# A two-layer decoder trunk: the out-projection's PSUM banks are filled with the residual ahead of the matmuls, the signs of the seven products are turned, and normed tiles are scaled whole

## The chip, the cores and the metric

The kernel runs on one core of a Trainium2 chip. The metric is the device time of one execution in microseconds (us), as the median of several runs. A profiled execution gives a trace beside it: every instruction of the engines with its start and duration, and every transfer with its issue and landing. The engines are TensorE (PE in the profile, PEld its weight loads), VectorE (DVE), ScalarE (ACT), GpSimd (POOL) and SyncE (SP), whose queue issues most loads.

## The reference

One sequence of 256 tokens with 2048 channels goes through two layers, all in float32. Cut to what matters:

```python
for l in range(DEPTH):                       # 2
    h = _rmsnorm(x, attn_norm_g[l])
    q, k, v, gate_b, gate_c, conv_in = jnp.split(h @ w_in[l], splits, axis=-1)   # 6 x 1024
    ...
    attn = _diff_attention(q, k, v, lam, rel_bias)       # then a norm per head
    conv = gate_b * _short_conv(gate_c * conv_in, conv_w[l])
    x = x + jnp.concatenate([attn, conv], axis=-1) @ w_out[l]
    hm = _rmsnorm(x, mlp_norm_g[l]) @ w_up[l]            # 2048 x 8192
    x = x + jnp.square(jax.nn.relu(hm)) @ w_down[l]      # 8192 x 2048
```

The change touches the norms, the projections of q and k, the out-projection (`w_out`) and the MLP.

## The kernel before

**Precision.** Every float32 operand is split into a high part and a rest (`hi`, `lo`), and a product is three matmuls: hi by hi, hi by lo, lo by hi. ScalarE makes the high part (a copy into the type that TensorE reads), VectorE the rest (a subtraction). For weights: a load (`raw`, `uraw`, `draw`), then `whi`/`uhi` (L341, L1291), then `wlo`/`ulo` (L342, L1292). For `w_up` one load of 1 MB holds two columns of 128 for half of k (`kh`), and is split in two steps, one for each column.

**Seven products.** At the indices listed in the plans (`FIRST`, `SECOND`, `LEFT`, `RIGHT`, `SEVEN_AT`) a 2 by 2 block of blocks is multiplied with seven products instead of eight. That needs sums of the activations' quarters (`sums_of`, L846: four VectorE operations of 128x128 into `sv`, then its hi and lo parts `sf`; in the MLP `square`, L1452 to L1455) and sums of the weights' quarters (`sums` in `jobs`, L910 to L924: `w7t`, four operations of 128x512; its first two are split into `w7x`, its last two into `w7y`; `w7b` is the split of the weights themselves). The products go into PSUM banks `prods[1]` to `prods[8]`; some of them end up in one block of the result and some are added in afterwards (`results`, L964 to L982).

**The out-projection.** Its left half (two chunks of 512 output channels, `left`) is worked beside the last columns of the gate, and the right half (`right`) follows. Banks `prods[2]`, `prods[3]`, `prods[4]`, `prods[8]` collect ordinary products and products of the seven. At the end VectorE adds each bank to the residual `xs` (L1061, L1167, four tiles of 128x512 per half), and four partial sums `e1` to `e4` to it (L980), after one addition straight from `prods[5]` (L975). The partial sums lie in a place of 4 KB of pool `tmp` (tag "ao"), one of `nat`, and one of `kpool` (tag "kL", 2 KB used).

**The norms.** `chunk` (L517) transposes a 512-channel tile of `xs` on TensorE, and, for pairs that aren't among the first sevens, `split_gained` (L304) makes hi on ScalarE (L307, scaled copy, 128x256) and lo on VectorE (L309). Of other pairs a scaled tile `ny` is made whole, then split (L540 to L543) and summed. `squares` (L555) makes the sums of squares on ScalarE (`junk`, L559).

**The MLP.** Column pair i of `w_up` is multiplied for both tokens' tiles (PE L1427: `up` is the first pair, `upw` the second, `upc` the rest), evicted, squared (`square`), and two pairs later multiplied with `w_down`. Its pools open where the pools of the attention part closed, so a load of `w_up` must wait until the last reader of that memory is done: the pools `upa`, `upb` and `upc` (L1269 on) take turns, and lie over `rpool`, `tmp`, `kpool` and others.

**Order.** TensorE's instructions are in program order. The other engines and SyncE's queue are ordered by the scheduler of the framework, which keeps the priority of the program and a model of when memory comes free; each queue is worked strictly in its order. `work.tick()` moves pieces of other work between matmuls; `late` and `issue_after` pin some instructions.

Of the kernel before, what the change touches and what calls it, by code (L numbers as in the profile page):

```python
# [133 lines left out]
def trunk(ctx: ExitStack, tc: tile.TileContext, x, w_in, w_out, conv_w, q_norm_g, k_norm_g,  # L134
# [370 lines left out]

    class Norm:
# [10 lines left out]
        def chunk(self, n, wait):  # L517
# [5 lines left out]
            for j in range(2):  # L523
# [9 lines left out]
                if self.sums_of is None or pair not in SEVEN_FIRST[self.l]:  # L533
                    split_gained(a, *((2 * j + i, tp[:, i * S:(i + 1) * S], scales[i])
                                      for i in range(2)))
                else:
                    y = wide(f"ny{pair}").rearrange("p (k s) -> p k s", k=2)
                    for i in range(2):
# [5 lines left out]
                    self.sums_of(pair, *(y[:, i, t * P:(t + 1) * P]  # L544
                                         for i in range(2) for t in range(NT)))
# [288 lines left out]
    A11, A21, A12, A22, S1, S2, S3, S4 = range(8)  # L834

    class BySeven:
# [9 lines left out]
        def sums_of(self, i, a11, a21, a12, a22):  # L846

            if i < self.rooms_of:
# [3 lines left out]
                hi, lo = (self.rooms[i % 2][:, part] for part in range(2))  # L852
            else:
# [11 lines left out]
        def jobs(self, w, i, cols, in_keys=False):  # L865
# [44 lines left out]
            def sums():  # L910
                left, right = mine["raw"]
                pool, tag = (self.kpool, "kL") if in_keys else (self.pool, "b")
                t = mine["t"] = pool.tile([P, 4, CH], F32, tag=tag, name="w7t")

                with behind(in_keys or self.rooms_of == 8):
                    nc.vector.tensor_sub(t[:, 0], right[:, 0], left[:, 0])
# [4 lines left out]
                nc.vector.tensor_add(t[:, 2], t[:, 1], left[:, 0])  # L921
                nc.vector.tensor_sub(t[:, 3], left[:, 1], t[:, 2])
                return made
# [7 lines left out]
        def form(self, i, pa, a):  # L931

            if a >= S1:
                return self.sums[i][pa][:, a - S1]
# [3 lines left out]
        def product(self, n, i, a, b, start, stop):  # L938

            for m, (pa, pw) in enumerate(TERMS):  # L940
                nc.tensor.matmul(self.prods[n], self.form(i, pa, a), b[pw],  # L941
                                 start=(start and m == 0), stop=(stop and m == 2))

        def pair(self, i, chunks, starts=(), last=False):

            for n, accs in chunks:
                hi, lo = self.weights.take()
                for j in range(2):
# [8 lines left out]
                    for t, pa, pw in steps:  # L957
# [3 lines left out]
                            stop=(last and j == 1 and (pa, pw) == TERMS[-1]))  # L961
                    work.tick()

        def results(self, n):  # L964
# [3 lines left out]
            x11, x21, x12, x22 = (xs[n + m][:, t] for m in range(2) for t in range(NT))  # L968
# [9 lines left out]
            def add():  # L978
                for x_, e in ((x11, e1), (x21, e3), (x12, e4), (x22, e3)):
                    nc.vector.tensor_add(x_, x_, e)  # L980

            return add  # L982
# [15 lines left out]
        def left(self, acts, cv):  # L998
# [8 lines left out]
            def column(c):  # L1007
# [8 lines left out]
                if c % 2 and i in SEVEN_LEFT + SEVEN_RIGHT:  # L1016
                    self.sums_of(i, *(y[:, k, t * P:(t + 1) * P]
                                      for k in range(2) for t in range(NT)))

            def banks():  # L1020
# [3 lines left out]
                for n in (5, 7, 4):  # L1024
                    prods[n] = bank(f"po{l}{n}")

            for j, (what, i) in enumerate(LEFT):
# [4 lines left out]
                elif what == "a":  # L1032
# [5 lines left out]
                    self.product(2, i, A12, b21, start, not {"a", 0} & rest)  # L1038
                    self.product(3, i, S4, b22, start, not {"a", 1} & rest)
                    self.product(5, i, S1, self.t1, start, end)  # L1040
                    work.tick()
                elif what == "b":
# [5 lines left out]
                    if end:  # L1048
                        add = self.results(0)
                else:  # L1050
                    opening = what == 1 and 8 not in prods
                    if opening:
                        prods[8] = ps.tile([P, CH], F32, tag="av", name=f"po{l}8", bufs=1)
# [699 lines left out]
```

## Time and profile before

| | |
|---|---|
| median of 3 runs | 2112.55 us (2112.5 to 2112.66) |
| span of the profiled execution | 2110.7 us |
| TensorE busy | 2105.2 us |
| VectorE busy | 1834.6 us |
| ScalarE busy | 1407.5 us |
| GpSimd busy | 189.4 us |
| read from and written to HBM | 440.52 MB and 33.58 MB |

The span runs from the first instruction of the profiled execution to its last; the page gives no other time of that execution, and the median of the runs stands 1.85 us above it. A row of the timeline gives the start and the duration of an instruction in us, its engine and line, what it writes and reads, and in brackets how long the engine sat idle before it and what ended that. A row of the groups gives the total busy time in us and the mean in ns, then the idle time before them. The chain that ended last is followed back from the last instruction to what released each.

### The profile page before, as it was taken

The numbers are of one execution on the slowest core, as the hardware profiler recorded it, in microseconds if no ns is written. First come the engines' busy times: TensorE is split into PE (matmuls) and PEld (weight loads), VectorE is DVE, ScalarE is ACT, GpSimd is POOL, SyncE is SP. The second block draws the span as 40 slices with busy tenths as digits, with TensorE's granted clock in tenths as the row PEclk, the third lists the DMA queues.
The fourth block names the chain that finished last, engine by engine and source line by source line (L and its number), as shares of the span: only waits on it lengthen the run. The fifth ranks groups of instructions, "written<-read, shape, count | busy, mean of one in ns | idle before, by whom it ended". The sixth has DMA issues, their size and how long they took to land.

```text
span 2110.7 us, 29252 instructions
## 1 busy us (share of the span) xinstructions
PE 2105.2 (100%) x10809; PEld 1799.0 (85%) x10809; DVE 1834.6 (87%) x2525; ACT 1407.5 (67%) x1823; POOL 189.4 (9%) x226
## 2 busy tenths in 40 slices
PE   9999999999999999999999999999999999999999
PEld 7888888888888888888888888888888888888887
DVE  7888788898888888799888887988988888888998
ACT  6777566676776766666566775657676677675664
POOL 2211120000000000011101121000000000000110
PEclk9999999999999999999999999999999999999999
DMA  7655575887777777789566456668777777777993
GB/s 265 205 154 167 171 216 182 289 259 229 230 238 229 231 232 230 251 291 310 171 220 188 152 170 185 195 193 290 255 238 229 229 230 238 230 229 260 315 309 113
DMA packets 312607, 476.01 MB, mean 226 GB/s; under 512 B 12723, under 2 KB 209669, under 8 KB 312464
## 3 DMA queue, kind: packets, MB, share of 16 engines
q1 hardware_dynamic: 284752, 406.76, 60.7%
q0 software_dynamic: 27520, 67.24, 10.1%
q8 instruction: 85, 1.39, 0.3%
q14 instruction: 58, 0.48, 0.1%
q10 hardware_dynamic: 192, 0.15, 0.0%
HBM read 440.52 MB, written 33.58 MB: 225 GB/s over the span
## 4 chain that ended last, share of the span: by engine, by line
PE 98%; DMA 1%; POOL 1%; DVE 1%; issue 0%; ACT 0%; ACTq 0%; DVEq 0%
PE upc L1427 31%; PE pr L1470 14%; PE dn L1551 8%; PE gc L481 4%; PE ci L481 4%; PE gb L433 4%; PE v L456 3%; PE q L958 3%; PE o L958 3%; PE k L958 3%; PE dn L1470 3%; PE po L941 2%; PE dn L1645 2%; PE pr1r L1470 2%; PE pr0r L1470 2%; PE po L958 2%
## 5 line engine op out<-in xcount | busy, mean ns | idle before, releaser
L1427 PE MATMUL upc<-nT,uhi 128*128 128x512 f32 x1920 | 454.7, 389 | 0.0
L1427 PEld LDWEIGHTS upc<-nT,uhi 128*128 128x128 f32 x1920 | 360.2, 188 | 74.7
L1292 DVE TENSOR_TENSOR ulo<-uraw,uhi 128x1024 fp32r<-128x1024 f32 x256 | 312.3, 1222 | 109.8 <-ACT f L1459 91.5
L341 ACT ACTIVATE whi<-raw 128x1024 fp32r<-128x1024 f32 x232 | 244.7, 1058 | 180.2 <-issue 21.8
L1291 ACT ACTIVATE uhi<-uraw 128x1024 fp32r<-128x1024 f32 x256 | 270.6, 1057 | 135.7 <-PE upc L1427 115.4
L342 DVE TENSOR_TENSOR wlo<-raw,whi 128x1024 fp32r<-128x1024 f32 x232 | 284.3, 1234 | 53.1 <-ACT whi L341 46.9
L1427 PEld LDWEIGHTS upc<-nT,ulo 128*128 128x128 f32 x1920 | 246.2, 191 | 9.4
L1427 PE MATMUL upc<-nT,ulo 128*128 128x256 f32 x1920 | 249.1, 283 | 0.0
L1317 ACT ACTIVATE bh<-draw 128x1536 fp32r<-128x1536 f32 x86 | 128.3, 1492 | 103.7 <-PE pr L1470 82.1
L1318 DVE TENSOR_TENSOR bl<-draw,bh 128x1536 fp32r<-128x1536 f32 x86 | 151.3, 1759 | 11.4 <-ACT bh L1317 10.9
L1551 PE MATMUL dn<-whi,fb 128*128 128x512 f32 x480 | 152.0, 389 | 0.0
L1470 PE MATMUL pr<-bh,f 128*128 128x512 f32 x360 | 121.4, 391 | 0.0
L341 ACT ACTIVATE whi<-uraw 128x1024 fp32r<-128x1024 f32 x60 | 63.7, 1062 | 72.0 <-PE dn L1551 58.5
L1437 ACT ACTIVATE ev<-upc 128x512 f32<-128x512 f32 x120 | 72.0, 600 | 54.0 <-PE upc L1427 54.0
L1317 ACT ACTIVATE t24h<-t 128x1024 fp32r<-128x1024 f32 x86 | 91.4, 1063 | 23.7 <-PE pr L1470 15.9
L1551 PEld LDWEIGHTS dn<-whi,fb 128*128 128x128 f32 x480 | 90.1, 188 | 18.6
L1318 DVE TENSOR_TENSOR t24l<-t,t24h 128x1024 fp32r<-128x1024 f32 x86 | 104.9, 1220 | 0.2
L1330 DVE TENSOR_TENSOR t<-draw 128x1024 f32<-128x1024 f32 x86 | 105.0, 1221 | 0.1
L1318 DVE TENSOR_TENSOR t13l<-t,t13h 128x1024 fp32r<-128x1024 f32 x86 | 104.9, 1220 | 0.0
L1317 ACT ACTIVATE t13h<-t 128x1024 fp32r<-128x1024 f32 x86 | 91.5, 1063 | 8.1 <-DVE t L1330 2.9
L1470 PE MATMUL pr<-t13h,f 128*128 128x512 f32 x240 | 93.8, 391 | 0.0
L1551 PE MATMUL dn<-wlo,fb 128*128 128x512 f32 x240 | 93.4, 389 | 0.0
(528 smaller groups left out, 4383.9 us busy)
## 6 DMA issues: line engine op xcount, KB each, us to landing
uraw<-in_w_up_dram SPq DMA_DIRECT2D x128, 1024.0 KB, 6.3
raw<-in_w_in_dram SPq DMA_DIRECT2D x191, 512.0 KB, 4.2
draw<-in_w_down_dram SPq DMA_DIRECT2D x180, 512.0 KB, 5.3
raw<-in_w_out_dram SPq DMA_DIRECT2D x64, 512.0 KB, 4.5
uraw<-in_w_down_dram SPq DMA_DIRECT2D x60, 512.0 KB, 6.8
hid0p<-f POOLq DMA_DIRECT2D x17, 512.0 KB, 3.5
fb<-hid0p POOLq DMA_DIRECT2D x17, 512.0 KB, 8.0
hid1p<-f POOLq DMA_DIRECT2D x17, 512.0 KB, 3.5
```

What stands on the lines that cost most here:

```text
L341: pair = (nc.scalar.activation(hi, raw, AF.Copy), nc.vector.tensor_sub(lo, raw, hi.bitcast(F32)))
L342: nc.vector.tensor_sub(lo, raw, hi.bitcast(F32)))
L481: nc.tensor.matmul(acc[:, f, 0] if part else acc[:, f], wt[:, k % 4, fs], a.ap[:, 0, k % KG] if part else a.ap[:, :, k % KG], start=(part ...
L958: nc.tensor.matmul(accs[t], a.ap[:, pa, k % KG, t * P:(t + 1) * P], (hi, lo)[pw][:, j], start=(j == 0 and (pa, pw) == (0, 0) and (n, t) in ...
L1291: pair = (nc.scalar.activation(hi, src, AF.Copy), nc.vector.tensor_sub(lo, src, hi.bitcast(F32)))
L1292: nc.vector.tensor_sub(lo, src, hi.bitcast(F32)))
L1317: keep(nc.scalar.activation(hi, src, AF.Copy))
L1318: keep(nc.vector.tensor_sub(lo, src, hi.bitcast(F32)))
L1330: keep(nc.vector.tensor_sub(t[:, 0:2], raw[:, 0::2], raw[:, 1::-1]))
L1427: nc.tensor.matmul(acc[:, 0] if part else acc, wt[part][:, k], a.ap[:, 0, k % KG] if part else a.ap[:, :, k % KG], start=(part == 0 and kh ...
L1470: nc.tensor.matmul(prods[n], f[:, pa, a], b[pw], start=(start and m == 0), stop=(stop and m == 2))
L1551: nc.tensor.matmul(prods[p], f[:, pa, 2 * k + t], b[pw][:, n], start=(p in starts and k == 0 and m == 0), stop=(stop and k == 1 and m == 2))
```

## The change

Five things are changed.

1. *Seeds.* ScalarE copies the residual `xs` into the out-projection's banks before their first matmul (`seed`), and these matmuls accumulate onto it (`start` false). The additions at the end are then `xs = bank + e`, and those of `xs` alone (L980, L975) go, except one for the left half.
2. *Room.* The partial sums of `results` lie in one place of 8 KB of `kpool` (tag "kL") in place of `tmp`.
3. *Signs.* The two sums S1 and S3 are turned so that the sums of quarters are two differences at one go, in `sums_of` and in the MLP's `square`: three operations in place of four (128x256 once, 128x128 twice). The weights' sums become additions. Where the signs of products 5, 6 or 7 turn, the additions of the results become subtractions.
4. *Order of w7t.* In q and k (`rooms_of == 8`) the last two sums of `w7t` are made before `w7x` is split.
5. *Norm tiles scaled whole.* All norms but the very first make `ny` and split it as one tile of 128x512: three copies on ScalarE and one subtraction on VectorE in place of two and two.

```diff
@@ class Norm, chunk @@
-                if self.sums_of is None or pair not in SEVEN_FIRST[self.l]:
+                if not at_once and (self.sums_of is None or pair not in SEVEN_FIRST[self.l]):
...
@@ class BySeven @@
-    A11, A21, A12, A22, S1, S2, S3, S4 = range(8)
+    A11, A21, A12, A22, S3, S1, S2, S4 = range(8)
...
-            nc.vector.tensor_add(v[:, 0], a21, a22)
-            nc.vector.tensor_sub(v[:, 1], v[:, 0], a11)
-            nc.vector.tensor_sub(v[:, 2], a11, a21)
-            nc.vector.tensor_sub(v[:, 3], a12, v[:, 1])
+            if both is None:
+                nc.vector.tensor_sub(v[:, 0], a11, a21)
+                nc.vector.tensor_sub(v[:, 1], a21, a22)
+            else:
+                nc.vector.tensor_sub(v[:, 0:2], *both)
+            nc.vector.tensor_sub(v[:, 2], v[:, 1], a11)
+            nc.vector.tensor_add(v[:, 3], a12, v[:, 2])
...
+                def rest():
+                    nc.vector.tensor_add(t[:, 2], t[:, 0], right[:, 1])
+                    nc.vector.tensor_add(t[:, 3], left[:, 1], t[:, 2])
+
                 with behind(in_keys or self.rooms_of == 8):
-                    nc.vector.tensor_sub(t[:, 0], right[:, 0], left[:, 0])
-                    nc.vector.tensor_sub(t[:, 1], right[:, 1], right[:, 0])
+                    nc.vector.tensor_add(t[:, 0], left[:, 0], right[:, 0])
+                    nc.vector.tensor_add(t[:, 1], right[:, 0], right[:, 1])
                 room = self.biasp.tile([P, 2, 2, CH], F32R, tag=self.spare, name="w7x")
+                if self.rooms_of == 8:
+                    rest()
                 made = two(room, t[:, 0:2])
...
+        def seed(self, *places):
+
+            for n, t, acc in places:
+                nc.scalar.activation(acc, xs[n][:, t], AF.Copy)
...
-            room = self.tmp.tile([P, 2, CH], F32, tag="ao", name="es", bufs=1)
-            e1, e2, e3 = room[:, 0], wide("e2"), room[:, 1]
-            e4 = self.kpool.tile([P, CH], F32, tag="kL", name="es4")
+            x21 = xs[n][:, 1]
+            room = self.kpool.tile([P, 4, CH], F32, tag="kL", name="es")
+            e1, e3, e4, e5 = (room[:, m] for m in range(4))
+            e2 = wide("e2")
             nc.scalar.activation(e1, prods[1], AF.Copy)
             nc.vector.tensor_add(e2, prods[6], e1)
-            nc.vector.tensor_add(e4, prods[5], e2)
-            nc.vector.tensor_add(x22, prods[5], x22)
+            nc.vector.tensor_sub(e4, prods[5], e2)
             nc.vector.tensor_add(e3, prods[7], e2)
...
+            nc.vector.tensor_sub(e5, prods[5], e3)
+            if n == 0:
+                nc.vector.tensor_add(x21, x21, e3)
+                e3 = x21
+            return (e1, e3), (e4, e5)
...
@@ right @@
+            for n in range(2):
+                self.seed(*((2 + n, t, accs[n][t]) for t in range(NT)))
...
                 if not {"s", what} & rest:
                     for t in range(NT):
-                        nc.vector.tensor_add(xs[2 + what][:, t], accs[what][t], xs[2 + what][:, t])
-                    if add is not None:
-                        add()
-                        add = None
+                        nc.vector.tensor_add(xs[2 + what][:, t], accs[what][t], e[what][t])
...
@@ mlp @@
-                    keep(nc.vector.tensor_sub(t[:, 0:2], raw[:, 0::2], raw[:, 1::-1]))
+                    keep(nc.vector.tensor_add(t[:, 0:2], raw[:, 1:3],
+                                              raw[:, 0:1].to_broadcast([P, 2, CH])))
...
-                    nc.vector.tensor_add(h[:, S1], h[:, A21], h[:, A22])
+                    nc.vector.tensor_sub(h[:, S3:S1 + 1], h[:, A11:A21 + 1], h[:, A21:A22 + 1:2])
                     nc.vector.tensor_sub(h[:, S2], h[:, S1], h[:, A11])
-                    nc.vector.tensor_sub(h[:, S3], h[:, A11], h[:, A21])
-                    nc.vector.tensor_sub(h[:, S4], h[:, A12], h[:, S2])
+                    nc.vector.tensor_add(h[:, S4], h[:, A12], h[:, S2])
```

In the left half banks 2 and 3 are seeded when they are opened (`banks`) and bank 8 when its first pair opens it; bank 4 is not, and the one addition to `xs` stands for it. The orders of TensorE and GpSimd are the same in both programs. Two places of the others follow, each before and after; the line numbers after are those of the changed file.

SyncE's queue from the last loads of `w_out` (`raw`) into the MLP of layer 0, before. `uraw` are loads of `w_up`, in the order pair 0 first half, pair 0 second half, pair 1 first half, pair 1 second half, pair 2 first half; `draw` are loads of `w_down`:

```order
L383 DMA raw<-in_w_out_dram 128x2x512 x10
L895 DMA raw<-in_w_out_dram 128x2x512 x2
L383 DMA raw<-in_w_out_dram 128x2x512 x2
L895 DMA raw<-in_w_out_dram 128x2x512 x2
L383 DMA raw<-in_w_out_dram 128x2x512 x4
L1284 DMA uraw<-in_w_up_dram 128x8x256 x5
L1302 DMA draw<-in_w_down_dram 128x1024 x6
L1284 DMA uraw<-in_w_up_dram 128x8x256 x5
```

And after, the same stretch:

```order
L383 DMA raw<-in_w_out_dram 128x2x512 x6
L1298 DMA uraw<-in_w_up_dram 128x8x256
L383 DMA raw<-in_w_out_dram 128x2x512 x4
L906 DMA raw<-in_w_out_dram 128x2x512 x2
L383 DMA raw<-in_w_out_dram 128x2x512 x2
L906 DMA raw<-in_w_out_dram 128x2x512 x2
L383 DMA raw<-in_w_out_dram 128x2x512 x4
L1298 DMA uraw<-in_w_up_dram 128x8x256 x3
L1316 DMA draw<-in_w_down_dram 128x1024 x3
L1298 DMA uraw<-in_w_up_dram 128x8x256
L1316 DMA draw<-in_w_down_dram 128x1024 x3
L1298 DMA uraw<-in_w_up_dram 128x8x256 x5
```

The second half of pair 1 has moved up among the loads of `w_out`; the three `uraw` are both halves of pair 0 and the first half of pair 2; the lone one between the `draw` is the first half of pair 1. The queue has the same order in layer 1.

VectorE at the first seven of q and k in layer 1, before:

```order
L916 TENSOR_TENSOR w7t<-raw 128x512
L917 TENSOR_TENSOR w7t<-raw 128x512
L880 TENSOR_TENSOR w7b<-raw,w7b 128x1024
L880 TENSOR_TENSOR wlo<-raw,whi 128x512
L921 TENSOR_TENSOR w7t<-w7t,raw 128x512
L880 TENSOR_TENSOR w7x<-w7t,w7x 128x1024
L922 TENSOR_TENSOR w7t<-raw,w7t 128x512
L342 TENSOR_TENSOR wlo<-raw,whi 128x1024
L880 TENSOR_TENSOR w7y<-w7t,w7y 128x1024
L342 TENSOR_TENSOR wlo<-raw,whi 128x1024
```

And after:

```order
L931 TENSOR_TENSOR w7t<-raw 128x512
L932 TENSOR_TENSOR w7t<-raw 128x512
L872 TENSOR_TENSOR sv_10049<-ny_10044,sv_10049 128x128
L891 TENSOR_TENSOR w7b<-raw,w7b 128x1024
L891 TENSOR_TENSOR wlo<-raw,whi 128x512
L927 TENSOR_TENSOR w7t<-w7t,raw 128x512
L874 TENSOR_TENSOR sf<-sv_10049,sf 128x512
L928 TENSOR_TENSOR w7t<-raw,w7t 128x512
L891 TENSOR_TENSOR w7x<-w7t,w7x 128x1024
L342 TENSOR_TENSOR wlo<-raw,whi 128x1024 x2
L891 TENSOR_TENSOR w7y<-w7t,w7y 128x1024
```

The fourth sum of `w7t` and the end of the other seven's sums (`sv`, `sf`) now stand ahead of `w7x`, and both `wlo` ahead of `w7y`.

More of the change, by code (lines that the diff above doesn't have):

```diff
@@ L504, in rstd_of, with quarters_of @@
         return r, power
+    def quarters_of(y):
+        q = y.rearrange("p k (t c) -> p (k t) c", c=P)
+        return *(q[:, m] for m in range(4)), (q[:, 0:2], q[:, 1:4:2])
     class Norm:
@@ L852, in sums_of @@
                 hi, lo = (self.rooms[i % 2][:, part] for part in range(2))
+            elif i % 2:
+                room = self.tmp.tile([P, 2, 4, P], F32R, tag="ao", name="so", bufs=1)
+                hi, lo = (room[:, part] for part in range(2))
             else:
@@ L1048, in left @@
                     if end:
-                        add = self.results(0)
+                        e = self.results(0)
                 else:
```

63 lines of the change are left out of this document (28 added, 35 removed).

## The prediction

> **What bounds the kernel now.** I read the page first: its busy times, the row of the granted clock and the chain that ended last.
>
> ```profile
> span 2110.7 us, 29252 instructions
> PE 2105.2 (100%) x10809; PEld 1799.0 (85%) x10809; DVE 1834.6 (87%) x2525; ACT 1407.5 (67%) x1823; POOL 189.4 (9%) x226
> PEclk9999999999999999999999999999999999999999
> PE 98%; DMA 1%; POOL 1%; DVE 1%; issue 0%; ACT 0%; ACTq 0%; DVEq 0%
> ```
>
> The reader is to see that TensorE is busy in 2105.2 of 2110.7 us, at the full granted clock in every slice, and that 98% of the chain is TensorE following itself. Next I asked for all waits of TensorE, which is a list of four:
>
> ```profile
> PE warm L189 <- DVE mhalf L181: 1.1, 1, 1.1
> PE q L958 <- ACT whi L368: 0.4, 1, 0.4
> PE tpb L570 <- DMA x<-in_x_dram: 0.2, 1, 0.2
> PE k00tp L688 <- DVE ke L660: 0.2, 1, 0.2
> ```
>
> They add up to 1.9 us in the whole span. The change leaves TensorE's instructions and their order as they are, so the most that removed waits can return is 1.9 us, which is 0.09% of the time. A measurement of this kernel can tell a difference of about 0.2%, 4.2 us, from none. The question is therefore whether a stall of more than 4.2 us appears. Last I read the chain around the places where instructions move, for the rate of TensorE:
>
> ```profile
> 359.73 5.44 PE o L958 x24
> ```
>
> 24 matmuls of 512 columns take 5.44 us, 0.2267 us each.
>
> **What costs nothing.** The change takes work off VectorE and puts some on ScalarE. Counted in the two programs, VectorE loses 130 operations of 128x128 and 44 scaled differences of the norm, and gains 65 of 128x256 and 8 of 128x512; ScalarE gains 36 copies of 128x512 (14 seeds, 22 in the norm). The groups:
>
> ```profile
> L1453 DVE TENSOR_TENSOR h<-h 128x128 f32<-128x128 f32 x60 | 17.2, 286 | 0.0
> L309 DVE SCALAR_TENSOR_TENSOR nT<-tpn,gains,nT 128x256 fp32r<-128x256 f32 x32 | 13.9, 478 | 1.1 <-ACT nT L307 1.1
> L980 DVE TENSOR_TENSOR x<-x,es 128x512 f32<-128x512 f32 x16 | 10.4, 685 | 0.0
> L559 ACT ACTIVATE junk<-x 128x512 f32<-128x512 f32 x32 | 19.8, 622 | 2.6 <-DVE e L1524 2.0 <-DVE x L980 0.6
> ```
>
> For a 128x256 operation I take 0.42 us, an estimate between 0.286 for 128 columns and 0.685 for 512. VectorE: 130 x 0.286 + 44 x 0.478 - 65 x 0.42 - 8 x 0.685 = 25 us less; ScalarE 36 x 0.622 = 22 us more. Neither sets the end, since TensorE waits for either only in the four rows above. That is the cover, and it must hold at each place. In the MLP, where 120 of the 128x128 operations turn into 60 of 128x256, it does: nothing is added on ScalarE, and there was no wait to remove.
>
> The seeds are new instructions that TensorE must wait for. A copy into PSUM I price at the 0.622 us of the copy above (bounds: 0.53, half of the 1.06 us of 1024 columns at 328.63 below, and 0.69, VectorE's 512-column add). The tightest are those of the right half of the out-projection and of bank 8:
>
> ```profile
> 315.58 5.44 PE po L958 x24
> 336.76 5.44 PE o L958 x24
> ...
> 315.75 0.63 ACT L879 ACTIVATE whi<-raw 128x512 fp32r<-128x512 f32 x1 [0.20 <-DMA raw<-in_w_out_dram]
> 328.63 1.06 ACT L341 ACTIVATE whi<-raw 128x1024 fp32r<-128x1024 f32 x1 [2.80 <-PE po L958]
> ...
> 336.31 1.88 DVE L1061 TENSOR_TENSOR x<-po,x 128x512 f32<-128x512 f32 x3
> ```
>
> Bank 8 opens half-way through the 24 matmuls at 315.58, at 318.3; its seed stands on ScalarE behind the split at 315.75, which ends at 316.4, so it is there at 317.0, 1.3 us early. The first two right seeds fit into the 2.80 us in which ScalarE idled before 328.63, 8 us before 336.76. The other two wait for banks that the adds at 336.31 free at 338.2 (and by then ScalarE has the four squares of 0.622 us to make); I put them at 339.6 and 341.3, and they are needed after the 24 matmuls and a group of transposes, at 342.6 at the earliest. At each place the slack is over 1.2 us; a seed at the dear end costs 0.07 us more. I count zero.
>
> **Term 1: the loads at the start of each MLP.** This is where the change costs. The four partial sums of `results` (L968) move out of their place in `tmp` into one 8 KB place of `kpool`. Memory of `tmp` comes free early, that of `kpool` late, and the uploads of the MLP's first weights use both. In the order of SyncE's queue one 1 MB load (of the second pair of columns, second half of k) goes forward among the loads of w_out; its partner, the first half of k, falls from third place to behind the load of the third pair and three loads of w_down. Before, these were (the answers for single loads: how long the issue took, when it was, how long to the landing):
>
> ```profile
> L1284 SPq DMA_DIRECT2D uraw<-in_w_up_dram x1: 367/367/367, 370.0 to 370.0; - x1
> DMA to landing us min/median/max: 6.6/6.6/6.6
> ...
> L1284 SPq DMA_DIRECT2D uraw<-in_w_up_dram x1: 367/367/367, 372.8 to 372.8; - x1
> DMA to landing us min/median/max: 9.2/9.2/9.2
> ...
> L1284 SPq DMA_DIRECT2D uraw<-in_w_up_dram x1: 367/367/367, 379.7 to 379.7; - x1
> DMA to landing us min/median/max: 5.9/5.9/5.9
> ...
> L1284 SPq DMA_DIRECT2D uraw<-in_w_up_dram x1: 368/368/368, 380.7 to 380.7; - x1
> DMA to landing us min/median/max: 8.3/8.3/8.3
> ...
> L1302 SPq DMA_DIRECT2D draw<-in_w_down_dram x6: 424/481/1532, 381.5 to 385.1; - x6
> DMA to landing us min/median/max: 8.7/9.8/11.9
> ```
>
> The first load, at 370.0, takes 6.6 us. The load in question is issued at 372.8 and lands at 382.0. Those at 379.7 and 380.7 land at 385.6 and 389.0, 3.5 apart, both being in flight; the six of w_down land from 381.5 + 8.7 = 390.2 to 385.1 + 11.9 = 397.0, 1.36 us apart. Who uses what:
>
> ```profile
> 376.66 1.06 ACT L1291 ACTIVATE uhi<-uraw 128x1024 fp32r<-128x1024 f32 x1 [2.91 <-DMA uraw<-in_w_up_dram]
> 387.58 1.06 ACT L1291 ACTIVATE uhi<-uraw 128x1024 fp32r<-128x1024 f32 x1 [0.23 <-PE up L1427]
> ...
> 379.50 1.22 DVE L1292 TENSOR_TENSOR ulo<-uraw,uhi 128x1024 fp32r<-128x1024 f32 x1
> 380.86 1.29 DVE L1167 TENSOR_TENSOR x<-o,x 128x512 f32<-128x512 f32 x2
> ...
> 393.99 3.82 PE L1427 MATMUL upw<-nT,uhi 128*128 128x512 f32 x16
> ```
>
> Its split into uhi (1.06 us) ran at 387.58, and TensorE used it at 393.99: 5 us in hand. After, ScalarE makes both squares (`junk`) between the first two splits, so VectorE's second difference moves from 379.50 to about 380.0 and ends at 381.2, which releases the load of the third pair. With nothing ahead of it in flight it should take about as long as the two fastest, 5.9 and 6.6, say 6.3: landing at 387.5. Three loads of w_down at 1.36 bring 391.6, and the load in question, 1 MB or two such steps, lands at 394.3 (its own memory, which holds the partial sums until the last adds, about those at 380.86 with 1.29 us, now ending at 382.3, is free before its turn). Split in 1.06, TensorE starts at about 395.35: 1.35 us late. The layer has a second, smaller delay in the same stretch: norm tiles are scaled whole, so the last lo half of the normed tiles comes later, about 0.5 us over its due time. That lies ahead of the same wait and vanishes in it. The cheap end: 5.9 and steps a tenth of a us shorter give 393.4 and a stall of 0.5; the dear end: 6.6, steps a tenth longer and the 3.5 for the 1 MB give 395.7 and 2.8. I take the middle, since the queue is full behind the first load as it was in the rows. Layer 1 has the same order of loads; two layers make 2.7 us. What stands behind the waiting split on ScalarE is the partner's split and the first split of w_down, both due over 1 us after.
>
> **Term 2: the first seven of layer 1.** In q and k the two later sums of `w7t` now stand ahead of the differences of w7x:
>
> ```profile
> 1078.72 0.69 DVE L916 TENSOR_TENSOR w7t<-raw 128x512 f32<-128x512 f32 x1 [0.73 <-DMA raw<-in_w_in_dram]
> 1079.93 1.22 DVE L880 TENSOR_TENSOR w7b<-raw,w7b 128x1024 fp32r<-128x1024 f32 x1
> 1085.22 1.23 DVE L880 TENSOR_TENSOR w7y<-w7t,w7y 128x1024 fp32r<-128x1024 f32 x1
> ...
> 1083.80 0.68 PE po1r L941 x3
> ```
>
> VectorE starts at a landing, 1078.72, so earlier savings don't help. Two 512-column operations lie between the first two rows, 1.21 us, so one starts 0.6 after another, 0.08 before its 0.685 are over; with the same overlap it is 1.14 for 1024 columns and 0.2 for 128. The new order: two sums 1.2, one 128-column sum 0.2, w7b 1.14, half of wlo 0.6, third sum 0.6, the low half of sf 0.6, fourth sum 0.6, w7x 1.14, two wlo 2.28, and w7y ends 1.23 after it starts: 1088.3. TensorE wants it with the 17th matmul after 1083.80, at 1083.80 + 16 x 0.2267 = 1087.4. Stall 0.9 us (0 if one wlo slips behind, 1.3 if ScalarE's whi for the second wlo is late).
>
> **Term 3: the seven of layer 0** was late already:
>
> ```profile
> 41.16 1.22 DVE L880 TENSOR_TENSOR w7y<-w7t,w7y 128x1024 fp32r<-128x1024 f32 x1
> 41.96 1.20 PE L941 MATMUL po0r<-w7y,sf 128*128 128x512 f32 x3
> 38.53 1.04 ACT L879 ACTIVATE w7y<-w7t 128x1024 fp32r<-128x1024 f32 x1
> ```
>
> The second of its three matmuls was due 0.2267 after 41.96, at 42.2, and the low half came at 42.4. ScalarE now makes w7y (before at 38.53) behind a copy of about 0.6 us and a split that waits for TensorE, which ends it at some 41.1 and the low half at 42.7: 0.3 us more (0 to 0.6).
>
> The sum is 2.7 + 0.9 + 0.3 = 3.9 us; against the span of 2110.7 that is 2114.6. The profile gives its execution's span alone, and the median of the runs, 2112.55, stands 1.85 us above it; with that, 2116.4. The bounds are 2 x 0.5 = 1.0 and 2 x 2.8 + 1.3 + 0.6 = 7.5 us, so 2113.5 to 2120.
>
> **The rivals.** *The load is in time.* If the load in question doesn't queue behind the others' bytes but takes the shortest time in the rows from its own issue (some 384.3: after 381.2, one issue of 1.53 and three of about 0.5 us), it lands at 384.3 + 5.9 = 390.2, is split by 391.3, and term 1 is zero: 2112.55 + 1.2 = 2113.75. For it: the load at 379.7 took 5.9 us though that of 372.8 was still in flight. Against: six loads of w_down landed 1.36 apart and waited up to 11.9 us.
>
> The Trainium skill, "SBUF — State Buffer", section "The DMA setup-cost knee", fits a load's time as about 2 us and its bytes over 436 GB/s; by it a 1 MB load takes an estimated 4.4 us, the landings come earlier and this rival holds. The trace disagrees, with 5.9 us for the fastest of these rows.
>
> *The load is later: slower.* The place is the same, the first upw of each MLP. If the landing is at 395.7 (the dear end), the two layers lose 5.6 and all is 2112.55 + 5.6 + 1.2 = 2119.35. It decides from 4.2 us in all, which is a stall of 1.5 us in each layer, a landing at 394.45 instead of 394.3. For it: this is hardly later than my estimate, and landings 3.5 apart occur. Against: with nothing in flight ahead of it the first load should be at the fast end.
>
> *VectorE's relief counts: faster.* If only waits go, 1.9 us at most: 2110.65, within 0.2%. Should TensorE's row hide waits for VectorE, up to the 25 us taken from it could return: 2087.5. Against it: 0.2267 us per matmul in 24 at 315.58, 336.76 and 359.73 alike, whatever VectorE did beside.
>
> The Trainium skill, "Perfetto Trace Analysis", section "Identifying the Most-Contended Engine", calls the busy share of matmuls a poor measure, and judges by the weight loads. By that rule the 85% of PEld would leave room for this rival; the even rate in the trace speaks against it.
>
> **How the numbers follow.** Forecast, with the middle sizes: 0.42. Load in time: 0.14. Load later: 0.38. Relief within the four waits: 0.04, beyond them: 0.02. Faster by over 0.2% is the last, 0.02; slower by over 0.2% is the third, 0.38; within 0.2% is the rest, 0.60. The likeliest is 2116.4. From 2112.6 to 2120 all but the relief (0.06) and the upper end of the late load (about 0.1) lie inside.
>
> **What would show it.** Right: in the waits of TensorE of the changed kernel new rows of upw on ACT uhi, about 1.35 us, twice; a row of po1r on DVE w7y of 0.9; PE's busy time unchanged; the load of term 1 landing near 394.3, about 10 us after issue. Wrong: upw starts right behind up without a gap; or a wait of TensorE at a place not named here, on a seed above all; or a chain with less than 2105 us of TensorE.

## The result and the profile after

The changed kernel takes 2123.85 us, median of 4 runs (2123.08 to 2124.59). The kernel before took 2112.61 us in the same session (2112.5 to 2114.92). The ratio is 1.0051, with an interval of 1.0039 to 1.0064: slower, by 11.2 us. Forecast were 2116.4 us and "within 0.2%", with a range up to 2120; the rival "the load is later" stood at 2119.35. The time lies outside the range, above both. The profiled execution took 2123.08 us, its span is 2121.3 us, 10.6 more than the 2110.7 of before.

The page of the changed kernel, in the rows that were shown of before:

```profile
span 2121.3 us, 29160 instructions
...
PE 2107.0 (99%) x10809; PEld 1798.5 (85%) x10809; DVE 1817.7 (86%) x2424; ACT 1422.5 (67%) x1859; POOL 188.1 (9%) x226
...
PEclk9999999999999999999999999999999999999999
```

TensorE has the same matmuls at the same clock; of the 1.8 us more that it counts as busy (2105.2 before), 1.3 come from the way the waits are read, as said below. VectorE has 16.9 us less to do (1834.6 before) and ScalarE 15 more, and none of that relief returned. Nearly all the new time is waiting. The waits of TensorE (engine, tile and line that waited, what it waited for; us in total, times, longest) were four rows with 1.9 us before and are now:

```profile
PE upw L1442 <- ACT uhi L1305: 2.8, 2, 1.4
PE po1r L957 <- DVE w7y L891: 1.7, 1, 1.7
PE po0r L957 <- DVE w7y L891: 1.5, 1, 1.5
PE po1r L957 <- DVE w7x L891: 1.2, 1, 1.2
PE up L1442 <- DVE nT L548: 1.1, 2, 0.6
PE warm L189 <- DVE mhalf L181: 1.1, 1, 1.1
PE po1r L957 <- DVE w7b L891: 0.7, 1, 0.7
PE q L975 <- ACT whi L368: 0.4, 1, 0.4
PE tpb L575 <- DMA x<-in_x_dram: 0.4, 1, 0.4
```

They add up to 10.9 us. The list counts from the modelled end of a matmul, 0.39 us after its start, while the next could have started after 0.227; so each wait costs 0.16 us more than its row, counted as busy. With eight new waits, 10.9 - 1.9 + 8 x 0.16 = 10.3 of the 10.6 us are found. By place: the starts of the two MLPs (upw, nT) 2.8 + 1.1 + 4 x 0.16 = 4.5 us; the first seven of layer 1 (`po1r`) 1.7 + 1.2 + 0.7 + 3 x 0.16 = 4.1; the first seven of layer 0 (`po0r`) 1.5 + 0.16, less the 0.2 that it lost before, 1.4. Forecast were 2.7, 0.9 and 0.3.

**The MLP's start.** The chain of waits of the changed kernel holds the load in question as a piece of its own (start, us, what):

```profile
385.91 10.47 DMA uraw<-in_w_up_dram
397.57 11.40 PE upw L1442 x64
```

The mechanism is the one forecast: this load now stands behind the load of the third pair and three loads of `w_down`, and TensorE waits for its split. It took 10.47 us (10 forecast) and landed at 396.4; in layer 1 the chain has it with 10.71 us, from 1441.59. The 24 matmuls of the out-projection that started at 359.73 before are in this chain

```profile
361.00 5.44 PE o L975 x24
```

so TensorE was 1.3 us behind already, and the landing is at 395.1 in before's time, not 394.3. In the same time `upw` starts at 396.3, 2.3 us after its 393.99 of before. TensorE's wait of 0.56 us for `nT`, at 391.5, lies ahead of this and doesn't move the landing, so at this place it is a part of the 2.3 and not an addition to it.

**The first seven of layer 1.** VectorE in the changed kernel (start, us, line, operation; in brackets the idle time before it and what ended it):

```profile
1071.46 0.16 DVE L587 TENSOR_REDUCE tot<-ss 128x2 f32<-128x8 f32 x1 [1.45 <-ACT junk L564]
...
1085.67 0.69 DVE L931 TENSOR_TENSOR w7t<-raw 128x512 f32<-128x512 f32 x1 [3.57 <-DMA raw<-in_w_in_dram]
```

The first of these rows in the kernel before:

```profile
1062.46 0.15 DVE L582 TENSOR_REDUCE tot<-ss 128x2 f32<-128x8 f32 x1
```

The squares that `tot` adds up are made on ScalarE (`junk`). In the changed kernel the last pair of them stands behind four copies of the norm (first fence); before, it started at 1060.94 (second fence):

```profile
1068.66 1.55 ACT L544 ACTIVATE ny<-tpn,ngains 128x256 f32<-128x256 f32 x4
1070.08 0.65 ACT L564 ACTIVATE junk<-x 128x512 f32<-128x512 f32 x1
```

```profile
1060.94 0.63 ACT L559 ACTIVATE junk<-x 128x512 f32<-128x512 f32 x1
```

Up to here TensorE has lost 1.4 us in layer 0 and half of the 4.5, 3.7 us together. The landing that starts `w7t` came at 1078.72 before and at 1085.67 now, so 3.3 us later than the stalls alone would put it; and `tot`, the end of the row's sum of squares, is 9.0 - 3.7 = 5.3 us late. GpSimd issues two bias loads (`rev`, 1 MB each) behind that row. GpSimd before:

```profile
1065.52 1.87 POOL L290 DMA_DIRECT2D rev<-by_dist_d  x2 [1.75 <-DMA raw<-in_w_in_dram]
```

and after:

```profile
1074.51 1.92 POOL L290 DMA_DIRECT2D rev<-by_dist_d  x2 [1.26 <-PE k L975]
```

They are 9.0 - 3.7 = 5.3 us late too, and now run beside the second of the two loads of the seven. For this load the profile says, in the changed kernel and before (how long the issue took, when it was, how long to the landing):

```profile
L906 SPq DMA_DIRECT2D raw<-in_w_in_dram x1: 368/368/368, 1077.1 to 1077.1; - x1
DMA to landing us min/median/max: 8.5/8.5/8.5
```

```profile
L895 SPq DMA_DIRECT2D raw<-in_w_in_dram x1: 367/367/367, 1073.1 to 1073.1; - x1
DMA to landing us min/median/max: 5.6/5.6/5.6
```

Before, the first load, at 1068.9, ran beside the bias loads and took 8.4 us, with time in hand, and the second, at 1073.1, took 5.6. After, the one at 1074.6 takes 3.9 and the one at 1077.1, on which `w7t` waits, 8.5.

**The first seven of layer 0.** GpSimd in the changed kernel, then VectorE beside it:

```profile
37.77 2.73 POOL L501 TENSOR_SCALAR row_e<-tot 128x2 f32<-128x2 f32 x1 [25.39 <-DVE tot L587]
```

```profile
37.49 1.21 DVE L342 TENSOR_TENSOR wlo<-raw,whi 128x1024 fp32r<-128x1024 f32 x1
38.63 0.68 DVE L928 TENSOR_TENSOR w7t<-raw,w7t 128x512 f32<-128x512 f32 x1
39.23 1.22 DVE L891 TENSOR_TENSOR w7x<-w7t,w7x 128x1024 fp32r<-128x1024 f32 x1
41.34 0.17 DVE L590 COPY rowf<-row_r 128x2 f32<-128x2 f32 x1 [0.89 <-POOL row_r L503]
...
42.56 1.22 DVE L891 TENSOR_TENSOR w7y<-w7t,w7y 128x1024 fp32r<-128x1024 f32 x1
```

and GpSimd before:

```profile
37.44 0.19 POOL L501 TENSOR_SCALAR row_e<-tot 128x2 f32<-128x2 f32 x1 [25.43 <-DVE tot L582]
```

The same two-column operation takes 0.19 us before, where VectorE idled from 37.25 to 37.70, and 2.73 after, where VectorE ran without a gap from 37.49 to 40.45. It ends at 40.50, as VectorE falls idle. VectorE itself works in order and waits for `row_r`, which GpSimd makes from that result (at `rowf`), and `w7y`, for which TensorE waits, stands behind that.

### The profile page after: what moved, and what is told of

Same layout as the page of the kernel before. It is cut to its first block, busy times and chain, and to the rows that moved or that the text cites. A ratio compares the mean times of both kernels' runs of the same rounds, so it can differ in the third digit from the quotient of the medians.

```text
span 2121.3 us, 29160 instructions
## 1 busy us (share of the span) xinstructions
PE 2107.0 (99%) x10809; PEld 1798.5 (85%) x10809; DVE 1817.7 (86%) x2424; ACT 1422.5 (67%) x1859; POOL 188.1 (9%) x226
## 4 chain that ended last, share of the span: by engine, by line
PE 96%; DMA 2%; ACT 1%; DVE 1%; issue 0%; POOL 0%; ACTq 0%; DVEq 0%; POOLq 0%; SPq 0%
PE upc L1442 31%; PE pr L1484 14%; PE dn L1567 8%; PE gc L481 4%; PE ci L481 4%; PE gb L433 4%; PE v L456 4%; PE o L975 3%; PE q L975 3%; PE k L975 3%; PE dn L1484 3%; PE po L957 2%; PE dn L1661 2%; PE pr1r L1484 2%; PE pr0r L1484 2%; PE po L975 2%
## 5 line engine op out<-in xcount | busy, mean ns | idle before, releaser
L1332 DVE TENSOR_TENSOR bl<-draw,bh 128x1536 fp32r<-128x1536 f32 x86 | 151.2, 1758 | 13.0 <-ACT bh L1331 10.6
```

The costliest lines, as they stand in the source:

```text
L1332: keep(nc.vector.tensor_sub(lo, src, hi.bitcast(F32)))
```

## Experiments

The theory after the result has three causes: **the room** (with the fourth partial sum, which the seeds need, the sums hold memory of the load at the MLP's start), **the norm** (tiles scaled whole put copies on ScalarE ahead of the row's squares, which moves the bias loads), and **the signs** (VectorE's new order starves GpSimd in layer 0). The rival is the prediction's: the new order of the sums of `w7t` makes the sevens late. All runs compute the whole reference; ratios are to the kernel before, which took 2112.42 to 2112.59 us in these sessions.

**The norm undone.** In the changed kernel:

```diff
-                if not at_once and (self.sums_of is None or pair not in SEVEN_FIRST[self.l]):
+                if self.sums_of is None or pair not in SEVEN_FIRST[self.l]:
```

> The changed kernel with one part undone: the norms make hi and lo straight from the transposed bank again (two copies, two scaled differences), except at the first sevens. Theory: the norm tiles scaled whole fill ScalarE at the start of layer 1, so its splits, the releases of the loads' places and the last squares come late, and the bias loads that stand behind the squares run into the loads of the first seven; that is 3 to 4 of the 4.5 us lost at the first seven of layer 1. In the MLP the waits of up for nT (2 x 0.7 us) go, but the waits of upw grow by the same, since the late load of w_up doesn't move. So about 3.5 us less than the changed kernel: 2120 us, with upw waits of 2.1 us each. Rival, the order of w7t is what costs in layer 1: then only the nT waits change and the time stays within 1 us of 2123.9. Rival, the nT delay is a stall of its own: 1.4 us more come back, 2118.8.

Measured: 2132.77 us, ratio 1.0099 (1.0085 to 1.0112); the profiled execution took 2135.11. Its waits:

```profile
PE upw L1442 <- ACT uhi L1305: 6.0, 2, 3.3
PE pr L1484 <- DVE t13l L1332: 5.0, 2, 2.5
PE po0r L957 <- DVE w7y L891: 1.5, 1, 1.5
```

All waits of the layer 1 sevens and both of nT are gone, which is the norm's part; but the time rose. The load at the MLP's start was issued at 386.56, took 11.47 us and landed at 398.0; the stall there grew to 3.3 us, and behind it the clock fell. A stretch of this run (us; busy us of PE, PEld, DVE, ACT, POOL with counts; granted clock, DMA share, GB/s):

```profile
399.40:404.80 5.40, 5.40 (x13) 4.25 (x14) 5.40 (x6) 4.97 (x6) 0.00 (x0) 0.50 0.76 254
```

13 matmuls of 512 columns in 5.40 us, at a clock of 0.50, where 24 take 5.44. Behind the stalls at `t13l` it is the same, 0.51 from 425.8 to 429.3. The expectation let each wait of `upw` grow to 2.1 us, but had neither a later landing nor the waits for `t13l` nor the clock. Why the load comes later without the norm's part is not shown.

**The order of `w7t` undone** (its two later sums behind the differences of w7x again):

```diff
-                if self.rooms_of == 8:
-                    rest()
                 made = two(room, t[:, 0:2])
-                if self.rooms_of != 8:
-                    rest()
+                rest()
```

> The changed kernel with one part undone: in q and k the last two sums of w7t stand behind the split of w7x again. Theory: it gives back the lateness of layer 0's seven (1.4 us late now against none: about 1.1 us) and less than 1 us of the 4.5 us in layer 1: 2122 us. Rival, this order is behind both places: 5 to 6 us come back, 2118. Rival, it costs nothing and layer 0's seven is late for ScalarE's other work: 2123.9.

Measured: 2128.03 us, ratio 1.0072 (1.0059 to 1.0085), so 4.2 us slower than the changed kernel. The rival falls: the new order is a gain. By the waits it is one in layer 0, where two waits for `w7y` (1.5 and 1.3 us) stand in place of one of 1.5; at the sevens of layer 1 they add up to 3.3 us, against 3.6 in the changed kernel. The clock falls behind both places (0.55 from 47.5 to 50 us, 0.50 from 1098 to 1102), where it stays at 1.00 in the changed kernel.

**The room undone.** The partial sums go back onto the tiles of the residual that are about to be overwritten, so the 8 KB place of `kpool` isn't used:

```diff
-            room = self.kpool.tile([P, 4, CH], F32, tag="kL", name="es")
-            e1, e3, e4, e5 = (room[:, m] for m in range(4))
+            e1, e3, e4, e5 = (xs[n + m][:, t] for m in range(2) for t in range(NT))
...
```

> The changed kernel with the partial sums of the out-projection kept in the residual's own tiles, which are free once the banks are seeded, so that they take no place of kpool. In the queue both halves of pair 1 of w_up then go forward among the loads of w_out. Theory: the place of the partial sums is the whole cause of upw's waits (1.4 us by the list, 1.5 and 1.6 us by the distance of the matmuls); the nT waits of 0.7 us stay: 3.1 us less, 2120.8 us, no wait of upw left. Rival, the loads at the MLP's start are late because of the norm's ScalarE work and not of that place: upw waits stay, 2123.9. Rival, w_up's loads ahead take bandwidth from w_out's and move the stall into the right half of the out-projection: between.

Measured: 2119.81 us, ratio 1.0036 (1.0023 to 1.0049). Both halves of the load are now issued early, at 324.0 and 326.6, and upw no longer waits; the waits at the sevens stand (`w7y` of layer 1 again 1.7), and so do those for nT:

```profile
PE up L1443 <- DVE nT L548: 1.1, 2, 0.6
```

The span is 3.3 us shorter than that of the changed kernel, 2.8 + 2 x 0.16 = 3.1 of it the two waits; by the medians the difference is 4.0.

**The room and the norm undone:**

> Partial sums in the residual's tiles and norms split from the bank; the order of w7t stays as the change has it. Theory: what remains is the one wait for w7y in layer 0, 1.4 us more than before: 2113.8 us, 3 us less than with the old order of w7t, which is then a gain of the change and no cost. Rival, without the norm's delay the loads of the MLP's start get later, as in e1_norm_two: waits of upw and of t13l come back, 2117 and more.

Measured: 2114.08 us, ratio 1.0008 (0.9999 to 1.0016), so hardly to be told from the kernel before. Of the new waits one is left:

```profile
PE po0r L957 <- DVE w7y L891: 1.5, 1, 1.5
```

Room and norm are 9.8 of the 11.2 us. **With the order of `w7t` undone as well:**

> All three undone or replaced: partial sums in the residual's tiles, norms split from the bank, old order of w7t. What is left of the change are the seeds and the turned signs. Theory: seeds and signs cost TensorE nothing and save it nothing, and the three others are the whole loss: 2112.5 us, within 0.2% of before (up to 1.9 us less). Rival, the seeds on ScalarE cost something themselves: slower than before by the part that then remains, and waits of PE for the banks' seeds in the list. Rival, the parts don't add up because each place is late for two reasons at once: some of the waits at w7y, w7x or up remain, 2114 to 2118.

Measured: 2116.79 us, ratio 1.0022 (1.0013 to 1.0031): 2.7 us dearer than with the new order, which confirms the second run without the other stalls around it. By the waits all of it lies in layer 0: with this order too there is no wait at the sevens of layer 1, and in layer 0 there are two of 1.4 us, the clock falling behind them (0.54 from 45 to 47.5).

**The parts one by one, from the kernel before.** First the turned signs and merged sums alone, without the seeds:

```diff
-                    nc.vector.tensor_sub(t[:, 0], right[:, 0], left[:, 0])
-                    nc.vector.tensor_sub(t[:, 1], right[:, 1], right[:, 0])
+                    nc.vector.tensor_add(t[:, 0], left[:, 0], right[:, 0])
+                    nc.vector.tensor_add(t[:, 1], right[:, 0], right[:, 1])
...
```

> The kernel before with one part of the change alone: the turned signs and the sums merged to one 128x256 operation; no seeds, old place of the partial sums, old order of w7t, norms as before. Theory: the 4.4 us that the kernel with all three parts undone still loses lie in the seven of layer 0 and come from the turned signs, which let the scheduler put VectorE's work there in another order; the seeds cost nothing. Then this kernel has the same two waits for w7y in layer 0 and takes 2116.8 us. Rival, the seeds or the room in the residual's tiles cost the 4.4 us: 2112.5 us, no such waits.

Measured: 2117.01 us, ratio 1.0020 (1.0012 to 1.0029), the time of the run before, which has the seeds in addition. Its new waits are much like those of that run (two of 1.4):

```profile
PE po0r L948 <- ACT w7y L886: 1.5, 1, 1.5
PE po0r L948 <- DVE w7y L887: 1.2, 1, 1.2
```

So the seeds cost nothing that can be told, and what is left there, in layer 0, belongs to the signs and merged sums; GpSimd's operation of layer 0 takes 2.73 us here too. Then the norm alone:

```diff
-                if self.sums_of is None or pair not in SEVEN_FIRST[self.l]:
+                if not at_once and (self.sums_of is None or pair not in SEVEN_FIRST[self.l]):
...
```

> The kernel before with the whole-scaled norm tiles alone. Theory: this part alone costs the 4 us at the first seven of layer 1 (late bias loads) and 2 x 0.7 us of up waiting for nT in the MLPs, no wait of upw and none in layer 0: 2118 us. Rival, the 4 us need the order of w7t too: then w7y there waits little, 2114. Rival, the nT waits hide nothing and cost nothing: 2116.6.

Measured: 2122.11 us, ratio 1.0043 (1.0029 to 1.0057), more than expected. Its waits:

```profile
PE po1r L942 <- ACT w7y L880: 2.6, 1, 2.6
PE up L1428 <- DVE nT L543: 1.1, 2, 0.6
...
PE po1r L942 <- DVE w7y L881: 0.9, 1, 0.9
PE po1r L942 <- DVE w7b L881: 0.6, 1, 0.6
```

and GpSimd's bias loads:

```profile
1071.82 1.87 POOL L290 DMA_DIRECT2D rev<-by_dist_d  x2 [1.26 <-PE k L959]
```

The norm alone, in the old program, makes the waits at the layer 1 sevens and both of nT. It moves the bias loads by 6.3 us. TensorE is 1.0 us late there (the transposes `tpn` that start at 1052.80 before start at 1053.79); 5.3 are the norm's own, as many as in the changed kernel. The waits come to 5.2 us, with 5 x 0.16 to 6.0; most of the rest of the 9.5 is the clock, 0.74 from 1090 to 1094 us and 0.50 from 1094 to 1098. Last, three partial sums, as before, in an 8 KB place of `kpool` (the activations' sums of odd indices take the freed place of `tmp`, as they do in the change):

```diff
+            room = self.kpool.tile([P, 4, CH], F32, tag="kL", name="es")
+            e1, e3, e4 = (room[:, m] for m in range(3))
...
```

> The kernel before with the partial sums in the 8 KB place of kpool alone (three of its four quarters used, and the sums of odd sevens in the freed place of tmp). In the queue the second half of pair 1 goes forward as in the change, but its first half stays ahead of all loads of w_down. Theory: no wait of upw, since only the fourth partial sum, which the seeds need, puts the load behind the others: 2112.5 us, the same as before. Rival, the place as such is enough: 3 us slower, 2115.6.

Measured: 2112.59 us, ratio 1.0000 (0.9991 to 1.0009). The place alone does nothing. That it takes the fourth sum, which the seeds need, to hold the load back is what remains by comparison with the run without the place; no run adds that sum alone.

**The bias loads moved behind the sevens.** On top of the version with the room undone, GpSimd reads an element of `w7t` before it issues the bias loads of layer 1, so that they can't run beside the second load; everything else, the norm too, stays as changed:

```diff
+                seen = small.tile([P, 1], F32, tag="seen", name="seen", bufs=1)
+                probe = nc.gpsimd.tensor_copy(seen, first.summed[0][:, 1, 0:1])
+                behind.enter_context(tc.issue_after(probe.ins))
...
```

> As e5_inplace (the norm tiles still scaled whole), with one thing moved: in layer 1 GpSimd issues its two 1 MB loads of the bias only when the first two sums of w7t of the first seven are made, so behind the landing of that seven's own weights. Theory: the norm's extra work on ScalarE made the row's statistic late, and with it these two loads, which then ran beside the load of the seven's second half (8.5 us to landing, against 3.9 for its first): the waits for w7b, w7x and w7y of 4 us go nearly all, 2116 us, and that load lands about 4 us after its issue. Rival, the splits on ScalarE are late themselves, and free the loads' places late: the load is issued at the same time as before and waits at w7x and w7y stay, 2119 to 2120. Rival, the bias loads then collide with the second seven: a new wait there, 2118.

Measured: 2127.91 us, ratio 1.0072 (1.0058 to 1.0086). The waits at the sevens of layer 1 went but for one of 0.5 us, yet all matmuls of some stages came further apart. The chain has

```profile
362.35 5.60 PE o L983 x24
```

and with the room undone alone 5.44 us: 24 matmuls in 5.60 us instead of 5.44, at the same granted clock. The run had added one new tile of 4 bytes per partition, so it was repeated with the element put into a tile that was there:

```diff
+                probe = nc.gpsimd.tensor_copy(fill[:, 0:1], first.summed[0][:, 1, 0:1])
```

> As e9_bias_gate, with the probe's one number written to a constant tile that is there anyway, and not to a new tile of 4 bytes. In e9_bias_gate the waits at the first seven went as the theory said (one of 0.5 us is left), but all of TensorE's 512-column matmuls of two stages started 232 and 229.5 ns apart on average where every other kernel has 227, which made 8 us. Theory: the 4 bytes moved every tile behind them to other addresses, and the time between matmuls depends on that; without them it is 227 again, and the time is that of e5_inplace less 3.5 us: 2116.3. Rival, the later bias loads or the waiting GpSimd slow TensorE: 232 ns again, 2127.9.

Measured: 2116.28 us, ratio 1.0017 (1.0009 to 1.0026), 3.5 us less than with the room undone alone. The 24 matmuls take 5.44 us again. The first of the two loads of the seven takes 3.8 us, and the second:

```profile
L912 SPq DMA_DIRECT2D raw<-in_w_in_dram x1: 367/367/367, 1075.8 to 1075.8; - x1
DMA to landing us min/median/max: 4.0/4.0/4.0
```

Neither load is slow now, and of the 3.5 us of waits at the layer 1 sevens (1.7 + 1.2 and a `w7b` of 0.6) 0.6 is left. The bias loads are the cause of the late landing.

**The row's copy behind `w7y`.** On top of room and norm undone, VectorE's copy `rowf` of layer 0 is put behind the low half of `w7y`:

```diff
-            nc.vector.tensor_copy(self.r, r)
+            with ExitStack() as behind:
+                if first:
+                    behind.enter_context(tc.issue_after(self.first.splits[3].ins))
+                nc.vector.tensor_copy(self.r, r)
...
```

> As e6_inplace_norm, with one VectorE instruction moved: in layer 0 the copy of the row's factor (rowf, which waits for GpSimd) stands behind w7y's low half and not ahead of it. Theory: in layer 0 VectorE, in order, waits 0.89 us for GpSimd with w7y behind it; moved, w7y ends about 1.1 us earlier, the wait for w7y falls from 1.7 to 0.5 us or less, 2112.7 us. On why GpSimd's row_e takes 2.73 us there and 0.19 in the kernel before: if GpSimd can't get on while VectorE works without a gap, row_e now takes longer still, until VectorE first idles (at about 42.7, so some 4 to 5 us); if it is slow by itself, for instance after its long pause, it stays at 2.73. Rival to the whole: w7y is late for ScalarE's order, and the time stays that of e6_inplace_norm.

Measured: 2113.02 us, ratio 1.0004 (0.9995 to 1.0013). TensorE's wait, then GpSimd and VectorE:

```profile
PE po0r L964 <- DVE w7y L897: 0.5, 1, 0.5
```

```profile
37.77 5.00 POOL L501 TENSOR_SCALAR row_e<-tot 128x2 f32<-128x2 f32 x1 [25.27 <-DVE tot L587]
```

```profile
41.51 1.22 DVE L897 TENSOR_TENSOR w7y<-w7t,w7y 128x1024 fp32r<-128x1024 f32 x1
```

`w7y` comes 1.05 us earlier, `rowf` follows at 43.61, and the wait drops from 1.5 to 0.5. The medians are 1.1 us apart, within the spread of these runs; it is the wait that shows the step. GpSimd's operation now takes 5.00 us, since VectorE has no gap until 42.73, and ends at 42.77. With seeds, signs and merged sums in place this version ties with the kernel before. It removes all but 0.5 us of what the change added; as no wait of note is left to remove, no version here beats the kernel before.

## Why the prediction was wrong

- *TensorE bounds the kernel and the relief returns nothing*: right. VectorE and ScalarE moved by 17 and 15 us (25 and 22 forecast) with no gain, and the 24 matmuls still take 5.44 us. *The seeds cost zero*: right; no row of the waits names one, and the runs with and without them agree (2116.79 and 2117.01 us).
- *Term 1, the load at the MLP's start*: mechanism right, size low. The step that was short is the first of its sum: the load of the third pair was taken at 6.3 us, "at the fast end", and took 7.2 from its issue at 382.3. With it the landing came at 395.1 in before's time instead of 394.3, and `upw` started 2.3 us late instead of 1.35; in both layers 4.5 instead of 2.7. That the lateness of the normed tiles "vanishes" in the same wait held as long as the load is late; where the load is early (the run with the room undone) the waits for nT stay and cost 1.1 + 2 x 0.16 us.
- *Term 2, the first seven of layer 1*: wrong in its cause. The step that failed is "VectorE starts at a landing, 1078.72, so earlier savings don't help". A landing was treated as a fixed time, while it hangs on what else is in flight. The norm's copies on ScalarE, which "What costs nothing" counted as covered, delay the row's squares, these GpSimd's bias loads, and these the landing by 3.3 us: 4.1 us of stalls instead of 0.9. And the new order of `w7t`, charged with the 0.9, makes no wait in layer 1 once room and norm are undone, and saves 2.7 us, in layer 0.
- *Term 3, the seven of layer 0*: 1.4 instead of 0.3. The prediction watched ScalarE, whose `w7y` ended at 41.27, close to the 41.1 forecast; the low half came at 43.78 instead of 42.7, because VectorE stood behind GpSimd's row.
- *The rival "the load is later"* named the right side, and in the MLP the right place: the landing, 395.1, is past the 394.45 from which it decides, though short of its 395.7. The time lies beyond it all the same. Most of the excess over the forecast lies in the two sevens, (4.1 - 0.9) + (1.4 - 0.3) = 4.3 us, which the prediction priced near zero or put down to another engine.

Settled by runs are the room (e.g. 2123.85 to 2119.81), the norm (with the bias loads as its way in layer 1), the order of `w7t`, the signs in layer 0 and the place of the row's copy there. Only argued is how the whole-scaled norm makes nT 0.55 us late: the wait stands in every run with it and in none without. Open is why the turned signs change VectorE's order in layer 0.

## What to carry to other kernels

Work put on an engine that is off the critical path is free only if nothing downstream is issued by its result: follow it through the semaphores to the next DMA issue, and ask which transfers that issue will then run beside. A landing time in a profile is not a constant; it belongs to the mix in flight. Where several small stalls are expected, change one part at a time: undoing one can make another worse. And a stall can cost more than its length: after the one of 3.3 us, 13 matmuls took 5.40 us instead of 13 x 0.2267 = 2.95.

## What the runs showed of the hardware

- **GpSimd can starve behind VectorE.** The same two-column operation took 0.19 us beside an idle VectorE, and 2.73 and 5.00 us beside a busy one, ending when VectorE fell idle. The one-element copy in front of the bias loads (the run with the element in an existing tile) took 11.73 us and ended at 1093.85; VectorE had no gap from 1082.12 to 1093.81:

```profile
1082.12 11.73 POOL L291 COPY fill<-w7t 128x1 f32<-128x1 f32 x1 [10.20 <-DVE w7t L938]
```

  The Trainium skill, "SBUF — State Buffer", section "Who interferes with whom", says that VectorE and GpSimd share one pair of ports under an exclusive lock, and that a VectorE operation with two inputs in SBUF contends with a GpSimd operation that reads SBUF. The traces agree, and add that the block lasts over several VectorE operations in a row, not one.
- **Stalls near 3 us halve the clock for a while.** After 3.3 us without matmuls 13 came at half rate, and after one of 2.6 us in the run with the norm alone the clock was 0.50 for 4 us; after two of 1.5 and 1.2 us close together, in layer 0 of the run with the signs alone, the clock was 0.64 for 2.5 us, while the 1.2 and 1.7 us of the changed kernel in layer 1 left it at 1.00:

```profile
47.50:50.00 2.50, 2.50 (x9) 1.99 (x8) 1.61 (x3) 0.00 (x0) 0.00 (x0) 0.64 0.92 269
```

  The Trainium skill, "TensorE: Matmul & The Clock Gate", section "What's actually happening", puts the drop to half after an idle window of about 3.4 us; the trace has it after somewhat less.
- **A new tile of 4 bytes per partition cost 11.6 us.** With it, 24 matmuls took 5.60 us instead of 5.44; with the element in an existing tile they didn't (2127.91 and 2116.28 us). That it shifts the addresses of later tiles is the likely reason, but no run shows it; which of them matter stays open.
